# A hybrid decoder layer: projections on two blocks of 512 columns at once, with TensorE in program order

## The chip, the cores and the metric

The kernel runs on one core of a Trainium2 chip. The metric is the device time of one execution in microseconds. The engines are TensorE (PE; its weight loads are shown apart as PEld), VectorE (DVE), ScalarE (ACT), GpSimd (POOL) and SyncE (SP), which here issues nearly all transfers.

## The reference

One decoder layer on 256 tokens with a residual stream of 2048 features, all in float32:

```python
h = h + 0.5 * swiglu(rmsnorm(h, ffn1_norm), ffn1_w_gu, ffn1_w_down)          # width 5632
proj = rmsnorm(h, mix_norm) @ w_in                                            # u | v | z | x,B,C | dt
a_out = chunked_sgu(gelu(u), gelu(v), gm_v_norm, gm_w_s, gm_b_s)              # chunks of 128 tokens
m_out = mamba2_group(z, xbc, dt, conv_w, conv_b, dt_bias, a_log, d, norm)     # conv of 4, scan, gate, norm
h = h + concat([a_out, m_out]) @ w_out
h = h + memory_cross_attention(rmsnorm(h, xa_norm), rmsnorm(mem, mem_norm), w_q, w_kv, w_o)  # 4 heads, 256 memory tokens
h = h + 0.5 * swiglu(rmsnorm(h, ffn2_norm), ffn2_w_gu, ffn2_w_down)
return rmsnorm(h, final_norm)
```

u, v, z and x are 2048 columns each, B and C 1024 each.

## The kernel before

The weights are float32 in HBM and are used once. A tile `raw` of 1 MB (128 partitions, 4 rows of k, 512 columns) is loaded by SyncE; ScalarE casts it into `whi` (float32r, 128x1024 a cast) and VectorE subtracts to get the rest, `wlo`. The operand (the normed stream, or the hidden values) is kept split the same way, high parts of 256 tokens beside low parts, in four tiles named `xt_...`, `hid`, `at` and so on. Each product is three matmuls: high by high, high by low, low by high. There are three buffers for `raw` and four each for `whi` and `wlo`.

`proj_tok` puts tokens on the partitions of the result: one block of 512 columns at a time, one PSUM bank for each of the two token tiles; the operand is the stationary side, the weights the moving one (lines 147 to 149, 128x512). `proj_feat` puts features on the partitions (lines 164 to 167, 128x256): x, B and C of w_in, the queries and the keys. Six PSUM banks serve both as accumulators, two more ("side" tiles) everything else: transposes, the scan's matmuls, logits.

The code is written stage by stage, and a scheduler sets the order of the instructions on every engine when the kernel is built: it may move a matmul ahead of others that stand earlier in the program, where dependences allow. The stages are: FFN 1 in two halves (6 and 5 blocks of gate and up columns, `w_gu`, then `w_dn`); B, C and x of w_in with their convolution (`conv_silu`: VectorE `xin`, four taps on ScalarE and VectorE, ScalarE's silu into `xf`); v, with the scan woven in; u, with `make_mixed`; z; w_out; queries, keys and `attend`; values; w_o; FFN 2 and the final norm.

The places that the text below comes back to:

- `x_tokens(c, xfs)` (line 401) transposes the convolved x of block c back to tokens. It is called after the projection of the next block.
- `scan_start(t, j)` loads `dec` by a broadcast from HBM, subtracts (line 438), takes a minimum, an exponential and multiplies with `scores` (line 446). `scan_apply` does the matmuls `yp` (line 456), `st` and `yo` (line 477).
- `make_mixed` (lines 521, 522): eight matmuls of 128x512, each evacuated by VectorE with the norm's weight.
- `to_operand` (line 192 and after) transposes 512 columns and writes an operand tile, by ScalarE (`hi`) and VectorE (`lo`), when its inputs are ready.
- At the start the stream is loaded by blocks `h0` to `h3` of 512 columns, with a weight tile behind each of the first three, and `first_stats` takes the sums of squares after the first projection.
- At the end `finish(n)` weights block n; the fourth call also takes the norm of each token tile and issues its four stores. The last projection is called with `apart=2`: its last two groups of rows run token tile by token tile.

```python
for n in range(4):
    pd = proj_tok(w_dn, c_from * NC, hts, n * NC, apart=2 if closing and c_to == 11 and n == 3 else 0)
    residual(n, pd, 0.5)
    if c_to == 11:
        done(n)
```

Of the kernel before, what the change touches and what calls it, by code (L numbers as in the profile page):

```python
# [16 lines left out]
P = 128  # L17
D = 2048
S = 256
# [14 lines left out]
KG = 4  # L34
LOG1P_TERMS = 9

# columns of the packed per-partition parameters
# [8 lines left out]
def hybrid_layer(ctx: ExitStack, tc: tile.TileContext, x, mem, w_gu1, w_dn1, w_in, w_s, w_out,  # L46
# [12 lines left out]

    def slot(shape, dtype, name):  # L60
        return big.tile(shape, dtype, name=name, tag="slot")
# [38 lines left out]
    def load(w, r0, n0, pieces=1):  # L100
        raw = wraw.tile([P, KG, NC], F32, name="raw")
        src = w[r0:r0 + KG * P, n0:n0 + NC].rearrange("(k p) n -> p k n", p=P)
        st = KG // pieces
        for j in range(0, KG, st):
            nc.sync.dma_start(out=raw[:, j:j + st, :], in_=src[:, j:j + st, :])
        return raw

    last_hi = [None]

    def split(raw, behind=None):  # L110
        # behind: for each half, instructions of ScalarE and VectorE to queue it behind
        parts = []
        for j in range(0, KG, 2):
            hi = wsp.tile([P, 2, NC], F32R, name="whi")
            lo = wsp.tile([P, 2, NC], F32R, name="wlo")
            with ExitStack() as order:
                for ins in behind[j // 2] if behind else ():
                    order.enter_context(tc.issue_after(ins))
                last_hi[0] = nc.scalar.copy(out=hi, in_=raw[:, j:j + 2, :]).ins  # L119
                nc.vector.tensor_tensor(out=lo, in0=raw[:, j:j + 2, :], in1=hi.bitcast(F32), op=ALU.subtract)  # L120
            parts.append((hi, lo))
        return parts
# [3 lines left out]
    def load_split(w, r0, n0):  # L126
        key = (id(w), r0, n0)
        return split(*ready.pop(key)) if key in ready else split(load(w, r0, n0))

    # Operands in xts: tiles [P, KG, 2 * S] with the high parts of S tokens, then the low parts.  # L130
    def proj_tok(w, r0, xts, n0, apart=0):
        # the last `apart` groups run token tile by token tile
        ps = [mm.tile([P, NC], F32, name="acc") for _ in range(NT)]
        groups = [[g] for g in range(len(xts) - apart)]
        if apart:
            groups.append(list(range(len(xts) - apart, len(xts))))
        for gs in groups:
            parts = {g: load_split(w, r0 + g * KG * P, n0) for g in gs}
            order = [(t, g, k) for g in gs for k in range(KG) for t in range(NT)]
            if len(gs) > 1:  # L140
                order.sort()
            for t, g, k in order:
                hi, lo = parts[g][k // 2]
                first, last = g == 0 and k == 0, g == len(xts) - 1 and k == KG - 1
                xh = xts[g][:, k, t * P:(t + 1) * P]
                xl = xts[g][:, k, S + t * P:S + (t + 1) * P]
                nc.tensor.matmul(ps[t], lhsT=xh, rhs=hi[:, k % 2, :], start=first, stop=False)  # L147
                nc.tensor.matmul(ps[t], lhsT=xh, rhs=lo[:, k % 2, :], start=False, stop=False)  # L148
                nc.tensor.matmul(ps[t], lhsT=xl, rhs=hi[:, k % 2, :], start=False, stop=last)  # L149
        return ps  # L150

    # Features on partitions: two tiles of [P, 2, S], for four groups of 128 features.
    def proj_feat(w, xts, n0):
        ps = [mm.tile([P, 2, S], F32, name="acc") for _ in range(2)]
        for g, xt in enumerate(xts):
            parts = load_split(w, g * KG * P, n0)
            for k in range(KG):
                hi, lo = parts[k // 2]
                first, last = g == 0 and k == 0, g == len(xts) - 1 and k == KG - 1
                for c in range(4):  # L160
                    cs = slice(c * P, (c + 1) * P)
                    o = ps[c // 2][:, c % 2, :]
                    # one accumulation group for both halves of a bank
                    nc.tensor.matmul(o, lhsT=hi[:, k % 2, cs], rhs=xt[:, k, :S], start=first and c % 2 == 0,  # L164
                                     stop=False)
                    nc.tensor.matmul(o, lhsT=hi[:, k % 2, cs], rhs=xt[:, k, S:], start=False, stop=False)  # L166
                    nc.tensor.matmul(o, lhsT=lo[:, k % 2, cs], rhs=xt[:, k, :S], start=False,  # L167
                                     stop=last and c % 2 == 1)
        return ps

# [14 lines left out]
    # 512 columns of NT token tiles -> one split operand tile, scaled per feature  # L185
    def to_operand(srcs, dst, c0=None):
        done = []
        for q in range(0, KG, 2):
            ps = side("tpose").rearrange("p (k s) -> p k s", k=2)
            for k in range(2):  # L190
                for t in range(NT):
                    nc.tensor.transpose(out=ps[:, k, t * P:(t + 1) * P],  # L192
                                        in_=srcs[t][:, (q + k) * P:(q + k + 1) * P], identity=ident)
            if c0 is None:
                hi = nc.scalar.copy(out=dst[:, q:q + 2, :S], in_=ps)
                lo = nc.vector.tensor_tensor(out=dst[:, q:q + 2, S:], in0=ps,
                                             in1=dst[:, q:q + 2, :S].bitcast(F32), op=ALU.subtract)
            else:
                for k in range(2):
                    sc = col[:, c0 + q + k:c0 + q + k + 1]  # L200
                    hi = nc.scalar.activation(dst[:, q + k, :S], ps[:, k, :], AF.Copy, scale=sc)
                    lo = nc.vector.scalar_tensor_tensor(out=dst[:, q + k, S:], in0=ps[:, k, :], scalar=sc,
                                                        in1=dst[:, q + k, :S].bitcast(F32),
                                                        op0=ALU.mult, op1=ALU.subtract)
            done.append((hi.ins, lo.ins))
        return done

    class Normed:
        """The next norm's operand, made chunk by chunk as the residual stream gets ready."""
# [5 lines left out]
        def chunk(self, n):  # L215
            self.operand(n)
            self.stats(n)

        def operand(self, n):
            dst = slot([P, KG, 2 * S], F32R, f"xt_{self.name}{n}")  # L220
            self.xts.append(dst)
            return to_operand([h[n][:, t, :] for t in range(NT)], dst, self.c0 + n * KG)
# [7 lines left out]
    def residual(n, ps, scale):  # L230
        for t in range(NT):
            nc.vector.scalar_tensor_tensor(out=h[n][:, t, :], in0=ps[t], scalar=scale, in1=h[n][:, t, :],
                                           op0=ALU.mult, op1=ALU.add)

# [1 line left out]
    def ffn(nrm, w_gu, w_dn, done, before=None, closing=False):  # L236
        for c_from, c_to in ((0, 6), (6, 11)):
            hts = []
            for c in range(c_from, c_to):
                pg = proj_tok(w_gu, 0, nrm.xts, c * NC)  # L240
                if c == 0 and before is not None:
                    before()
                gs = []
                for t in range(NT):
                    g = half_k(F32, "gate")
                    nc.scalar.activation(g, pg[t], AF.Silu, scale=nrm.rstd[:, t:t + 1])
                    gs.append(g)
                pu = proj_tok(w_gu, 0, nrm.xts, DFF + c * NC)
                for t in range(NT):
                    nc.vector.scalar_tensor_tensor(out=gs[t], in0=pu[t], scalar=nrm.rstd[:, t:t + 1],  # L250
                                                   in1=gs[t], op0=ALU.mult, op1=ALU.mult)
                dst = slot([P, KG, 2 * S], F32R, "hid")
                to_operand(gs, dst)
                hts.append(dst)
            for n in range(4):
                pd = proj_tok(w_dn, c_from * NC, hts, n * NC, apart=2 if closing and c_to == 11 and n == 3 else 0)
                residual(n, pd, 0.5)
                if c_to == 11:
                    done(n)

    n1 = Normed("ffn1", C_FFN1)
    for n in range(4):
        for t in range(NT):
            nc.sync.dma_start(out=h[n][:, t, :], in_=x_v[:, t, n * NC:(n + 1) * NC])
        if n < 3:
# [452 lines left out]
```

## Time and profile before

| | |
|---|---|
| median of 3 runs | 2558.9 us (2558.71 to 2560.08) |
| the profiled execution, span | 2557.8 us |
| TensorE busy | 2539.3 us, 99% |
| VectorE busy | 1375.6 us, 54% |
| ScalarE busy | 1164.2 us, 46% |
| HBM read | 472.57 MB, 186 GB/s over the span |

The span is the time from the first to the last instruction or transfer of one execution, which the profiler recorded; it is 1.1 us under the median of the runs that were timed without it. Matmuls overlap: a shown length holds the filling of the array too, so that the step from one start to the next is what a matmul costs. In a row of the timeline stand the start, the length, the engine, the line of the code, the operation, result and operands, the shape, how many were merged, and in brackets the idle time before it with what ended it.

### The profile page before, as it was taken

The numbers are of one execution on the slowest core, as the hardware profiler recorded it, in microseconds if no ns is written. First come the engines' busy times: TensorE is split into PE (matmuls) and PEld (weight loads), VectorE is DVE, ScalarE is ACT, GpSimd is POOL, SyncE is SP. The second block draws the span as 40 slices with busy tenths as digits, with TensorE's granted clock in tenths as the row PEclk, the third lists the DMA queues.
The fourth block names the chain that finished last, engine by engine and source line by source line (L and its number), as shares of the span: only waits on it lengthen the run. The fifth ranks groups of instructions, "written<-read, shape, count | busy, mean of one in ns | idle before, by whom it ended". The sixth has DMA issues, their size and how long they took to land.

```text
span 2557.8 us, 31301 instructions
## 1 busy us (share of the span) xinstructions
PE 2539.3 (99%) x12990; PEld 2160.8 (84%) x12990; DVE 1375.6 (54%) x1444; ACT 1164.2 (46%) x1391; POOL 19.8 (1%) x44
## 2 busy tenths in 40 slices
PE   8999999999999999999999999999999999999998
PEld 7888888888889998878888999888888888888887
DVE  5445444545557677755555555555554544445454
ACT  5444434444445455445444544444444443344443
POOL 0000000000000000000000000000000000000000
PEclk9999999999999999999999999999999999999999
DMA  6555555555555555545555655455555555555564
GB/s 236 193 183 193 185 197 196 182 191 188 184 175 173 185 189 190 196 158 190 194 185 182 214 180 167 148 181 177 185 187 192 191 187 194 191 191 189 198 192 145
DMA packets 238704, 476.73 MB, mean 186 GB/s; under 512 B 9713, under 2 KB 9873, under 8 KB 237793
## 3 DMA queue, kind: packets, MB, share of 16 engines
q1 hardware_dynamic: 236736, 465.86, 54.2%
q0 software_dynamic: 1680, 8.73, 1.1%
q8 instruction: 101, 1.65, 0.3%
q14 instruction: 43, 0.34, 0.0%
q10 hardware_dynamic: 144, 0.13, 0.0%
HBM read 472.57 MB, written 2.13 MB: 186 GB/s over the span
## 4 chain that ended last, share of the span: by engine, by line
PE 99%; DMA 0%; issue 0%; SPq 0%; ACT 0%; DVE 0%; ACTq 0%; POOLq 0%; POOL 0%
PE acc L147 27%; PE acc L148 27%; PE acc L149 27%; PE acc L164 5%; PE acc L166 5%; PE acc L167 5%; PE tpose L192 2%; PE yp L456 1%; DMA h<-in_x 0%; PE mixed L521 0%; PE o L654 0%; PE o L652 0%; PE scores L443 0%; PE logits L610 0%; PE logits L611 0%
## 5 line engine op out<-in xcount | busy, mean ns | idle before, releaser
L120 DVE TENSOR_TENSOR wlo<-raw,whi 128x1024 fp32r<-128x1024 f32 x880 | 1076.9, 1225 | 1100.6 <-ACT whi L119 1100.3
L119 ACT CAST whi<-raw 128x1024 fp32r<-128x1024 f32 x880 | 927.4, 1054 | 1253.3 <-PE acc L149 1095.8
L148 PE MATMUL acc<-wlo,xt_ffn 128*128 128x512 f32 x1408 | 550.2, 391 | 0.0
L149 PE MATMUL acc<-whi,xt_ffn 128*128 128x512 f32 x1408 | 550.1, 391 | 0.0
L147 PE MATMUL acc<-whi,xt_ffn 128*128 128x512 f32 x1408 | 548.8, 390 | 0.0
L148 PEld LDWEIGHTS acc<-wlo,xt_ffn 128*128 128x128 f32 x1408 | 264.6, 188 | 54.3
L147 PEld LDWEIGHTS acc<-whi,xt_ffn 128*128 128x128 f32 x1408 | 264.6, 188 | 54.3
L149 PEld LDWEIGHTS acc<-whi,xt_ffn 128*128 128x128 f32 x1408 | 264.7, 188 | 53.6
L148 PE MATMUL acc<-wlo,hid 128*128 128x512 f32 x704 | 274.6, 390 | 0.0
L149 PE MATMUL acc<-whi,hid 128*128 128x512 f32 x704 | 274.5, 390 | 0.0
L147 PE MATMUL acc<-whi,hid 128*128 128x512 f32 x704 | 274.0, 389 | 0.0
L148 PEld LDWEIGHTS acc<-wlo,hid 128*128 128x128 f32 x704 | 132.1, 188 | 27.4
L147 PEld LDWEIGHTS acc<-whi,hid 128*128 128x128 f32 x704 | 132.2, 188 | 27.3
L149 PEld LDWEIGHTS acc<-whi,hid 128*128 128x128 f32 x704 | 132.2, 188 | 26.8
L147 PE MATMUL acc<-whi,xt_mix 128*128 128x512 f32 x384 | 151.7, 395 | 0.0
L149 PE MATMUL acc<-whi,xt_mix 128*128 128x512 f32 x384 | 150.9, 393 | 0.0
L148 PE MATMUL acc<-wlo,xt_mix 128*128 128x512 f32 x384 | 150.0, 391 | 0.0
L164 PE MATMUL acc<-xt_mix,whi 128*128 128x256 f32 x512 | 145.5, 284 | 0.0
L166 PE MATMUL acc<-xt_mix,whi 128*128 128x256 f32 x512 | 145.2, 284 | 0.0
L167 PE MATMUL acc<-xt_mix,wlo 128*128 128x256 f32 x512 | 144.8, 283 | 0.0
L164 PEld LDWEIGHTS acc<-xt_mix,whi 128*128 128x128 f32 x512 | 98.2, 192 | 0.6 <-issue 0.4
L166 PEld LDWEIGHTS acc<-xt_mix,whi 128*128 128x128 f32 x512 | 98.2, 192 | 0.2
(237 smaller groups left out, 2827.7 us busy)
## 6 DMA issues: line engine op xcount, KB each, us to landing
raw<-in_w_gu SPq DMA_DIRECT2D x173, 1024.0 KB, 4.8
raw<-in_w_dn SPq DMA_DIRECT2D x88, 1024.0 KB, 5.1
raw<-in_w_in SPq DMA_DIRECT2D x80, 1024.0 KB, 5.1
raw<-in_w_out SPq DMA_DIRECT2D x32, 1024.0 KB, 5.2
raw<-in_w_kv SPq DMA_DIRECT2D x32, 1024.0 KB, 5.4
raw<-in_w_q SPq DMA_DIRECT2D x16, 1024.0 KB, 5.3
raw<-in_w_o SPq DMA_DIRECT2D x16, 1024.0 KB, 5.1
dec<-cum_rows POOLq DMA_DIRECT2D x4, 1024.0 KB, 5.7
```

The costliest lines, as they stand in the source:

```text
L119: last_hi[0] = nc.scalar.copy(out=hi, in_=raw[:, j:j + 2, :]).ins
L120: nc.vector.tensor_tensor(out=lo, in0=raw[:, j:j + 2, :], in1=hi.bitcast(F32), op=ALU.subtract)
L147: nc.tensor.matmul(ps[t], lhsT=xh, rhs=hi[:, k % 2, :], start=first, stop=False)
L148: nc.tensor.matmul(ps[t], lhsT=xh, rhs=lo[:, k % 2, :], start=False, stop=False)
L149: nc.tensor.matmul(ps[t], lhsT=xl, rhs=hi[:, k % 2, :], start=False, stop=last)
L164: nc.tensor.matmul(o, lhsT=hi[:, k % 2, cs], rhs=xt[:, k, :S], start=first and c % 2 == 0, stop=False)
L166: nc.tensor.matmul(o, lhsT=hi[:, k % 2, cs], rhs=xt[:, k, S:], start=False, stop=False)
L167: nc.tensor.matmul(o, lhsT=lo[:, k % 2, cs], rhs=xt[:, k, :S], start=False, stop=last and c % 2 == 1)
L192: nc.tensor.transpose(out=ps[:, k, t * P:(t + 1) * P], in_=srcs[t][:, (q + k) * P:(q + k + 1) * P], identity=ident)
L456: nc.tensor.matmul(yp[:, i, :], lhsT=dec[:, hh, :], rhs=xdt[:, j * 16 + hh, :], start=True, stop=True)
```

## The change

`proj_tok` now takes two blocks of 512 columns at once. For the FFN these are a gate block and its up block, elsewhere neighbours. It holds four accumulators, and a weight tile is 2 rows of k by 1024 columns (still 1 MB). In the first and the last piece the matmuls run token tile by token tile, and each token tile is evacuated (`evac`) as soon as it is complete. `add_proj` does so for the projections into the stream, so two blocks of `h` are completed together.

Every matmul and transpose on TensorE is kept in program order. Matmuls that belong to no projection are put off by `later(fn, by)`: they are emitted after so many further pieces (`step()` at the end of each piece of a projection).

```diff
+    steps, put_off = [0], []
+    def matmul(out, lhsT, rhs, start=False, stop=False):
+        return tc.keep_in_program_order(nc.tensor.matmul(out, lhsT=lhsT, rhs=rhs, start=start, stop=stop))
+    def later(fn, by=1):
+        put_off.append((steps[0] + by, len(put_off), fn))
+    def step(to=None):
+        steps[0] += 1
+        for job in sorted(put_off, key=lambda j: j[:2]):
+            if job[0] <= steps[0] or to == "end":
+                put_off.remove(job)
+                job[2]()
...
-    def proj_tok(w, r0, xts, n0, apart=0):
-        ps = [mm.tile([P, NC], F32, name="acc") for _ in range(NT)]
-        groups = [[g] for g in range(len(xts) - apart)]
...
-                nc.tensor.matmul(ps[t], lhsT=xh, rhs=hi[:, k % 2, :], start=first, stop=False)
-                nc.tensor.matmul(ps[t], lhsT=xh, rhs=lo[:, k % 2, :], start=False, stop=False)
-                nc.tensor.matmul(ps[t], lhsT=xl, rhs=hi[:, k % 2, :], start=False, stop=last)
+    def proj_tok(w, r0, xts, cs, evac, kts=D // P, apart=1):
+        n = kts // KP
+        groups = [[i] for i in range(n - apart)] + [list(range(n - apart, n))]
+        for ng, pieces in enumerate(groups):
+            parts = {i: load_split(w, r0 + i * KP * P, cs) for i in pieces}
+            order = [(t, i, k) for i in pieces for k in range(KP) for t in range(NT)]
+            if ng in (0, len(groups) - 1):
+                order.sort()
+            for t, i, k in order:
...
+                matmul(a, xh, hi[:, 0, :], start=first, stop=False)
+                matmul(a, xh, lo[:, 0, :])
+                matmul(b, xh, hi[:, 1, :], start=first)
+                matmul(b, xh, lo[:, 1, :])
+                matmul(a, xl, hi[:, 0, :], start=False, stop=last)
+                matmul(b, xl, hi[:, 1, :], stop=last)
+                if last:
+                    evac(t, ps[t])
+            step()
...
+    def add_proj(w, r0, xts, scale, done=None, **kw):
+        for n in range(0, 4, 2):
+            def evac(t, ps):
+                for j in range(2):
+                    hh = h[n + j][:, t, :]
+                    nc.vector.scalar_tensor_tensor(out=hh, in0=ps[j], scalar=scale, in1=hh, op0=ALU.mult, op1=ALU.add)
...
+            if done is not None:
+                done(n)
+                done(n + 1)
...
+    first = [(0, 0), (0, 1), (1, 2)]
...
+    for n in range(1, 4):
+        later(lambda n=n: x_operand(n), by=2 * n - 1)
+    for n in range(4):
+        later(lambda n=n: n1.stats(n), by=4 + n)
...
     for c in range(4):
         ps = proj_feat(w_in, nx.xts, X0 + c * NC)
-        if late is not None:
-            x_tokens(*late)
...
+            later(lambda c=c, i0=i0, xf=xf: x_tokens(c, i0, xf), by=1 + i0 // 2)
...
+    for i, (by, to) in enumerate(((3, 7), (7, 10), (13, 17), (17, 21))):
+        later(lambda i=i: scan_start(i // 2, i % 2), by=by)
+        later(lambda i=i: scan_apply(i // 2, i % 2), by=to)
...
+    for g in range(4):
+        later(lambda g=g: make_mixed(g), by=2 + g)
...
-    ffn(n2, w_gu2, w_dn2, finish, closing=True)
+    ffn(n2, w_gu2, w_dn2, finish, {"apart": 2})
+    step("end")
```

`first` says which weight tiles stand behind which block of x at the start: two behind `h0`, one behind `h1`. With `apart=2` the last two pieces (of 2 rows of k each) run token tile by token tile. `operand_later`, new too, puts the transposes of an operand tile off by one piece, half a tile each.

In the order of the instructions this shows at three places. The names with numbers are buffers; `xt_mix_...` are the operand tiles of the mixers' norm.

TensorE at the first block of x, before: the eight transposes stand behind the last matmul of the second block's projection.

```order
L167 MATMUL acc<-xt_mix_5085,wlo 128x256
L401 MATMUL tpose<-ident,xf 128x128 x8
L164 MATMUL acc<-xt_mix_4494,whi 128x256
L166 MATMUL acc<-xt_mix_4494,whi 128x256
L167 MATMUL acc<-xt_mix_4494,wlo 128x256
```

The same now: four transposes stand behind the first piece of the second block's projection (48 matmuls on the first operand tile).

```order
L69 MATMUL acc<-xt_mix_4805,whi 128x256 x2
L69 MATMUL acc<-xt_mix_4805,wlo 128x256
L72 MATMUL tpose<-ident,xf 128x128 x4
L69 MATMUL acc<-xt_mix_4815,whi 128x256 x2
L69 MATMUL acc<-xt_mix_4815,wlo 128x256
```

The transposes moved from the end of the next projection to the end of its first quarter. ScalarE around the same place, now (lines 374 and 378 are the convolution's, 148 the cast, 483 the copy of the transposes):

```order
L374 ACTIVATE cacc<-xin_5168,col 128x256
L148 CAST whi<-raw 128x1024 x2
L378 ACTIVATE xf<-cacc,col 128x256
L374 ACTIVATE cacc<-xin_5169,col 128x256
L374 ACTIVATE cacc<-xin_5167,col 128x256
L148 CAST whi<-raw 128x1024
L378 ACTIVATE xf<-cacc,col 128x256 x2
L374 ACTIVATE cacc<-xin_5168,col 128x256
L483 COPY y_6359<-tpose 128x256
```

Up to the last row this is the order of before; the copies of the transposes have come into it. VectorE at the very end, before (`h_81` to `h_84` are the four blocks of the stream, line 232 the addition, lines 180 and 181 the norm's mean, 679 and 681 the scaling):

```order
L232 SCALAR_TENSOR_TENSOR h_84<-acc,h_84 128x512
L180 TENSOR_REDUCE ms<-ss_f 128x1
L181 TENSOR_SCALAR ms<-ms 128x1
L679 SCALAR_TENSOR_TENSOR h_84<-h_84,rstd_f_19090,fw 128x512
L681 TENSOR_SCALAR h_83<-h_83,rstd_f_19090 128x512
L232 SCALAR_TENSOR_TENSOR h_84<-acc,h_84 128x512
L180 TENSOR_REDUCE ms<-ss_f 128x1
```

And now (lines 291, 223, 224, 770 and 772 are the same five; 764 multiplies the third block with the final norm's weight):

```order
L291 SCALAR_TENSOR_TENSOR h_84<-acc,h_84 128x512
L764 TENSOR_TENSOR h_83<-h_83,fw 128x512
L291 SCALAR_TENSOR_TENSOR h_83<-acc,h_83 128x512
L291 SCALAR_TENSOR_TENSOR h_84<-acc,h_84 128x512
L764 TENSOR_TENSOR h_83<-h_83,fw 128x512
L223 TENSOR_REDUCE ms<-ss_f 128x1
L224 TENSOR_SCALAR ms<-ms 128x1
L772 TENSOR_SCALAR h_83<-h_83,rstd_f_19269 128x512
```

The mean of token tile 0 moved behind the additions of token tile 1. ScalarE at the start, before and then now (line 201, now 242, writes the operand; 217 is a sum of squares):

```order
L201 ACTIVATE xt_ffn_129<-tpose,col 128x256 x3
L119 CAST whi<-raw 128x1024
L201 ACTIVATE xt_ffn_129<-tpose,col 128x256
L119 CAST whi<-raw 128x1024
L201 ACTIVATE xt_ffn_148<-tpose,col 128x256 x3
```

```order
L217 ACTIVATE junk,ss_ffn_111<-h_81 128x512 x2
L242 ACTIVATE xt_ffn_135<-tpose,col 128x256 x3
L217 ACTIVATE junk,ss_ffn_111<-h_82 128x512
L242 ACTIVATE xt_ffn_135<-tpose,col 128x256
L148 CAST whi<-raw 128x1024 x4
```

Sums of squares, the first of `h_82` among them, have moved ahead of the first cast.

More of the change, by code (lines that the diff above doesn't have):

```diff
@@ L153, in proj_feat @@
     def proj_feat(w, xts, n0):
         ps = [mm.tile([P, 2, S], F32, name="acc") for _ in range(2)]
[L155 to L159, printed above, removed]
+        for i in range(D // P // (2 * KP)):
+            raw = wraw.tile([P, 2 * KP, NC], F32, name="raw")
+            nc.sync.dma_start(out=raw, in_=w[2 * i * KP * P:2 * (i + 1) * KP * P, n0:n0 + NC].rearrange(
+                "(k p) n -> p k n", p=P))
+            parts = split(raw.rearrange("p (k j) n -> p k j n", j=2))
+            for k in range(2 * KP):
+                kt = 2 * i * KP + k
+                hi, lo = (x[:, k % 2, :] for x in parts[k // 2])
+                xt = xts[kt // KG][:, kt % KG, :]
+                first, last = kt == 0, kt == D // P - 1
@@ L162, in proj_feat @@
                     o = ps[c // 2][:, c % 2, :]
[L164 to L168, printed above, removed]
+                    matmul(o, hi[:, cs], xt[:, :S], start=first and c % 2 == 0, stop=False)
+                    matmul(o, hi[:, cs], xt[:, S:])
+                    matmul(o, lo[:, cs], xt[:, :S], start=False, stop=last and c % 2 == 1)
+            step()
         return ps
@@ L183, in rstd_of @@
         return r
[L186 to L189, printed above, removed]
-            for k in range(2):
[L191 to L206, printed above, removed]
@@ L208, in hybrid_layer, with operand_later, half, first @@
+    def operand_later(srcs, to, name, c0=None, by=1):
+        def half(q):
+            if q == 0:
+                to.append(slot([P, KG, 2 * S], F32R, name))
+            return to_operand(srcs, to[at], q, c0)
+        at = len(to) + sum(1 for o in owed if o is to)
+        owed.append(to)
+        def first():
+            owed.remove(to)
+            assert len(to) == at
+            half(0)
+            later(lambda: half(2), by=0)
+        later(first, by)
+    owed = []
     class Normed:
@@ L421, in hybrid_layer @@
     dend = small.tile([P, HEADS], F32, name="dend", bufs=1)
-    ecum = small.tile([P, HEADS], F32, name="ecum", bufs=1)
-    nc.scalar.activation(ecum, cum[:, 1, :], AF.Exp)
     scan = {}
@@ L463, in scan_apply @@
             nc.vector.tensor_tensor(out=xdt, in0=xdt, in1=per_head(dend, HD), op=ALU.mult)
-            scan["states"] = states = slot([P, GROUPS, REP * HD], F32, "states")
-            for q in range(4):
-                st = side("st").rearrange("p (g d) -> p g d", g=2)
-                for i in range(2):
-                    g = q * 2 + i
-                    nc.tensor.matmul(st[:, i, :], lhsT=btok[:, g, :], rhs=xdt[:, g * REP:(g + 1) * REP, :],
-                                     start=True, stop=True)
-                nc.any.tensor_copy(out=states[:, q * 2:q * 2 + 2, :], in_=st)
+            later(scan_states, by=2)
         else:
@@ L483, in scan_apply, with scan_states @@
                 nc.vector.tensor_tensor(out=ys, in0=ys, in1=tq, op=ALU.add)
+    def scan_states():
+        scan["states"] = states = slot([P, GROUPS, REP * HD], F32, "states")
+        xdt = scan["xdt0"]
+        for q in range(4):
+            st = side("st").rearrange("p (g d) -> p g d", g=2)
+            for i in range(2):
+                g = q * 2 + i
+                matmul(st[:, i, :], btok[:, g, :], xdt[:, g * REP:(g + 1) * REP, :], start=True, stop=True)
+            nc.any.tensor_copy(out=states[:, q * 2:q * 2 + 2, :], in_=st)
     wst = const.tile([P, 4, P], F32, name="wst")
@@ new lines, in hybrid_layer, with evac @@
+    for hd in (0, 2):
+        vvs = [slot([P, 2, 2, XD], F32R, "vv") for _ in range(2)]
+        def evac(m, ps):
+            for j in range(2):
+                nc.scalar.copy(out=vvs[j][:, m, 0, :], in_=ps[j])
+                nc.vector.tensor_tensor(out=vvs[j][:, m, 1, :], in0=ps[j], in1=vvs[j][:, m, 0, :].bitcast(F32),
+                                        op=ALU.subtract)
+        proj_tok(w_kv, 0, mem_ts, (D + hd * XD, D + (hd + 1) * XD), evac)
+        for j in range(2):
+            for q in range(2):
+                later(lambda hd=hd, j=j, q=q, vv=vvs[j]: weigh(hd + j, vv, q), by=1 + j)
```

415 lines of the change are left out of this document (208 added, 207 removed).

## The prediction

> **What bounds the kernel now.** I read the page first: busy shares, the chain that ended last, the costliest groups.
>
> ```profile
> span 2557.8 us, 31301 instructions
> PE 2539.3 (99%) x12990; PEld 2160.8 (84%) x12990; DVE 1375.6 (54%) x1444; ACT 1164.2 (46%) x1391; POOL 19.8 (1%) x44
> ...
> PE 99%; DMA 0%; issue 0%; SPq 0%; ACT 0%; DVE 0%; ACTq 0%; POOLq 0%; POOL 0%
> ...
> L120 DVE TENSOR_TENSOR wlo<-raw,whi 128x1024 fp32r<-128x1024 f32 x880 | 1076.9, 1225 | 1100.6 <-ACT whi L119 1100.3
> L119 ACT CAST whi<-raw 128x1024 fp32r<-128x1024 f32 x880 | 927.4, 1054 | 1253.3 <-PE acc L149 1095.8
> L148 PE MATMUL acc<-wlo,xt_ffn 128*128 128x512 f32 x1408 | 550.2, 391 | 0.0
> ...
> L148 PEld LDWEIGHTS acc<-wlo,xt_ffn 128*128 128x128 f32 x1408 | 264.6, 188 | 54.3
> ```
>
> TensorE is the chain. VectorE waits for the ScalarE cast, the cast waits for TensorE to release a buffer: both are about half idle, ahead of TensorE. The wide matmul groups have no idle before them. The list of TensorE's own waits has two lines, and only the first is of any size; it belongs to the start.
>
> ```profile
> PE tpose L192 <- DMA h<-in_x: 8.4, 2, 4.7
> PE tpose L626 <- DVE probs L622: 0.2, 1, 0.2
> ```
>
> So little waiting is left to remove. What a matmul costs is read from start to start, since the shown lengths overlap; the timeline, first and last of 55 matmuls:
>
> ```profile
> 599.63 0.39 PE L147 MATMUL acc<-whi,xt_ffn 128*128 128x512 f32 x1
> 599.86 0.39 PE L148 MATMUL acc<-wlo,xt_ffn 128*128 128x512 f32 x1
> 600.09 0.39 PE L149 MATMUL acc<-whi,xt_ffn 128*128 128x512 f32 x1
> ...
> 611.88 0.39 PE L147 MATMUL acc<-whi,xt_ffn 128*128 128x512 f32 x1
> ```
>
> (611.88 − 599.63)/54 = 0.2267 us. The change issues the same matmuls, so what it can alter is this spacing, the stalls in the middle (few, by the list above), the start and the tail.
>
> **The change, part by part.** The FFN, Z, w_out, w_o and the second half of w_kv: blocks of 1024 columns, 1 MB a piece, four accumulators. A piece is 24 matmuls, 24 × 0.2267 = 5.44 us, and needs two casts (2.1 us) and two subtractions (2.45 us): cover of more than half, as before. I take 0. The cover is the four wlo/whi buffers; should an evacuation at the end of a projection delay casts by more than about 3 us (5.44 − 2.45), this zero is gone (a rival below). The FFN's loads as two transfers of half the size and SP's longer list change nothing while the casts wait for TensorE and not for data.
>
> *X stage.* x_tokens(c) no longer stands one whole projection after its convolution, but one piece of the next one after it (its second half two pieces). TensorE now obeys program order, so it cannot run other matmuls meanwhile. Timeline after the first X projection, TensorE, then VectorE and ScalarE, then the transposes:
>
> ```profile
> 870.87 0.28 PE L164 MATMUL acc<-xt_mix,whi 128*128 128x256 f32 x1
> ...
> 872.19 0.28 PE L167 MATMUL acc<-xt_mix,wlo 128*128 128x256 f32 x1
> 872.31 0.28 PE L164 MATMUL acc<-xt_mix,whi 128*128 128x256 f32 x1
> ...
> 872.51 1.14 DVE L303 TENSOR_TENSOR xin<-acc,rstd_b 128x256 f32<-128x256 f32 x3
> ...
> 878.27 2.46 DVE L310 SCALAR_TENSOR_TENSOR cacc<-xin,col,cacc 128x256 f32<-128x256 f32 x6
> ...
> 878.93 1.05 ACT L119 CAST whi<-raw 128x1024 fp32r<-128x1024 f32 x1 [0.62 <-PE acc L166]
> 880.36 0.92 ACT L312 ACTIVATE xf<-cacc,col 128x256 f32<-128x256 f32 x2 [0.38 <-DVE cacc L310]
> ...
> 896.08 1.03 PE L401 MATMUL tpose<-ident,xf 128*128 128x128 f32 x8
> ```
>
> Narrow matmuls start every (872.31 − 870.87)/12 = 0.12 us. The projection ends at 872.31; its last matmul is the one of 872.19. The first half of x_tokens needs the xf of two convolutions: the second is the first of the pair at 880.36 and is done at about 880.36 + 0.51 = 880.87, 8.56 us after the projection's end. Before, the transposes came at 896.08, with 15 us to spare. Now TensorE reaches them after one piece, 48 × 0.12 = 5.76 us, and waits 8.56 − 5.76 = 2.8 us, three times; the fourth time V's first piece lies ahead, 5.44 us, and it waits 3.1. The order on ScalarE around it is unchanged, so I keep 8.56. Sum 3 × 2.8 + 3.1 = **+11.5** (8 to 14: each chain a microsecond shorter or longer). The second half, after two pieces, finds its xf ready.
>
> *V and U.* Program order now places scores, yp, st, yo and mixed at stated pieces. Before, this stage ran almost without a hole: in the window 1073.42 to 1096.08 (22.66 us) stand 33 wide matmuls (7.48 us), 32 passes of yp (3.5), 16 of yo, 16 of mixed and 8 transposes (0.9).
>
> ```profile
> 1073.42 3.52 PE yp L456 x32
> 1076.93 0.92 PE yo L477 x4
> 1078.79 1.73 PE yo L477 x8
> ...
> 1093.79 0.86 PE mixed L521 x2
> ```
>
> With 1.73/8 = 0.216 a yo pass and 0.86/2 = 0.43 a mixed pass that is 7.48 + 3.5 + 3.5 + 6.9 + 0.9 = 22.3, so only 0.4 us of hole. New holes I expect at two places. First, in U's second piece mixed needs both side banks, one of them held by the scores of the last scan step until VectorE has done the multiplication; the second half of mixed also waits for the first to be evacuated, and that stands on VectorE behind a dec subtraction, which waits for a broadcast that starts only when a slot is free:
>
> ```profile
> L438 DVE TENSOR_TENSOR dec<-dec,cum 128x2048 f32<-128x2048 f32 x4 | 9.2, 2292 | 0.5 <-DMA dec<-cum_rows 0.5
> L522 DVE TENSOR_TENSOR v<-mixed,wn 128x512 f32<-128x512 f32 x8 | 5.3, 684 | 2.2 <-PE mixed L521 2.2
> ...
> dec<-cum_rows POOLq DMA_DIRECT2D x4, 1024.0 KB, 5.7
> ```
>
> Landing 5.7 + subtraction 2.3 + evacuation 0.7 = 8.7 us after the slot is free, against one piece and a mixed, about 6.3: 2.4, with queueing 3. Second, the piece where the last mixed, yp and yo come together takes eight side tiles of 0.69 us of VectorE each, by two banks: about 2, and 1 for smaller ones. Less the about 2 us of holes that V and U have today: **+4** (0 to 8).
>
> *C0 and attention.* cum's copies now hold both side banks ahead of b_tokens: +0.2. Probabilities turn two pieces later than their logits: the 0.2 us wait of the list and some smaller ones go, −1 (−1 to 0).
>
> *Start.*
>
> ```profile
> 4.66 2.30 PE L192 MATMUL tpose<-ident,h 128*128 128x128 f32 x8 [4.66 <-DMA h<-in_x]
> ...
> 8.57 1.05 ACT L119 CAST whi<-raw 128x1024 fp32r<-128x1024 f32 x1 [0.21 <-DMA raw<-in_w_gu]
> ...
> 10.72 1.49 PE L192 MATMUL tpose<-ident,h 128*128 128x128 f32 x4 [3.76 <-DMA h<-in_x]
> ...
> 11.86 1.20 PE L147 MATMUL acc<-whi,xt_ffn 128*128 128x512 f32 x2
> ...
> 13.29 0.63 PE L149 MATMUL acc<-whi,xt_ffn 128*128 128x512 f32 x1
> 13.71 0.63 PE L148 MATMUL acc<-wlo,xt_ffn 128*128 128x512 f32 x1
> ...
> 15.33 0.39 PE L147 MATMUL acc<-whi,xt_ffn 128*128 128x512 f32 x1
> 15.56 0.39 PE L148 MATMUL acc<-wlo,xt_ffn 128*128 128x512 f32 x1
> ...
> 8.00:11.00 3.00, 0.28 (x1) 0.18 (x1) 2.08 (x4) 2.78 (x4) 0.00 (x0) 1.00 1.05 399
> ```
>
> The second block of x lands at 10.72 today, behind one weight tile; now behind two. 1.05 MB more at 399 GB/s is 2.6 us: 13.4. On ScalarE the sum of squares of that block now stands ahead of the fourth xt_ffn activation and of the first cast. So the first cast, at 8.57 today, begins at 13.4 + 0.8 + 0.5 = 14.7, and the first matmul at about 15.8 instead of 11.86: +3.9. TensorE is slow then (13.29 to 13.71 is 0.42, 0.23 from 15.3 on), as today, and four subtractions in a row follow: **+5** in all (2 to 7).
>
> *Tail.*
>
> ```profile
> 2546.37 7.21 SPq L684 DMA_DIRECT2D out<-h  x8
> 2548.11 0.39 PE L149 MATMUL acc<-whi,hid 128*128 128x512 f32 x1
> ...
> 2548.54 0.69 DVE L232 SCALAR_TENSOR_TENSOR h<-acc,h 128x512 f32<-128x512 f32 x1 [1.77 <-PE acc L149]
> ```
>
> Today token tile 0 is finished under the last matmuls and four of the eight stores go out early; the last is issued at 2546.37 + 7.21 = 2553.58, 5.2 us after the last matmul's slot (2548.11 + 0.23). Now two blocks end together, and on VectorE and ScalarE tile 0's row sum stands behind tile 1's additions and squares, which wait for the last matmul: two additions (1.4), a multiplication, two squares, then two chains of reduce, power and scaling, four multiplications, and all eight stores behind them. By my list the last store is issued about 8.3 us after: **+3.1** (2 to 5).
>
> Sum: 11.5 + 4 + 0.2 − 1 + 5 + 3.1 = +22.8. On the span of 2557.8 that is 2580.6; the median of the runs shown, 2558.9, is 1.1 above the span: 2581.7, so **2582 us**. With each part's bounds (8, 0, −1, 2, 2 and 14, 8, 0, 7, 5): 2570 to 2593.
>
> **Rivals.**
>
> *Faster: a weight kept in the array.* Today one of three matmuls has the stationary operand of its predecessor (L147 to L148); now four of six. If a repeat saved the part of the slot that does not scale with columns, 0.2267 − 2 × (0.2267 − 0.12) = 0.0133 us, then 9024 wide matmuls (by the code: the two FFNs 6336, V, U and Z 1152, w_out 768, values and w_o 768) × 0.0133 × (4/6 − 1/3) = 40 us would go and the time be about 2582 − 40 = 2542. Against it: L147 to L148 (0.23) repeats, L148 to L149 (0.23) doesn't, with the same step, and L148 has its own 1408 loads. I give it 0.05. It decides as soon as a repeat saves over 9 ns. The Trainium skill, "TensorE: Matmul & The Clock Gate", Part 2, step ①, says that decoupled loading allows to load once and multiply repeatedly, which speaks for this case; the equal steps show no gain from it here.
>
> *The X waits are hidden.* If the convolution's chain runs 3 us faster when its pieces come sooner, 11.5 goes: about 2570. For it: ScalarE idles before most casts; against: six VectorE steps of 2.46 and a cast stand in the chain itself. 0.10.
>
> *The clock falls after each X wait.* TensorE ran at 0.42 a wide matmul until 15.3, after 3.8 us of idleness ending at 10.72. If each of four waits of about 3 us set it back for the same 4.6 us (10.72 to 15.3), half of that is lost: 4 × 2.3 = 9, about 2591. 0.10. The Trainium skill, same page, "HAM oscillation — how this bites in real kernels", puts the limit at idle gaps of about 3.4 us; by it gaps of 2.8 and 3.1 just escape, and the sum stays.
>
> *Casts late at every projection.* One microsecond at each of the 44 pairs of blocks: +44, about 2626. Against: the half-idle ScalarE and VectorE. 0.05. It decides when evacuation and cast together exceed 5.44 us.
>
> *Nothing:* the new waits are as small as the old: about 2559. 0.04, as the list of TensorE's waits has no such gap to trade.
>
> **How the numbers follow.** Forecast 0.66, the others 0.05, 0.10, 0.10, 0.05, 0.04. The range 2566 to 2597 takes in the forecast, the hidden X waits and the clock, 0.86, less some edges. 0.2%, 5 us, is about what a measurement can tell from no change here: slower 0.91, same 0.04, faster 0.05.
>
> **What would show it.** In the list of TensorE's waits: tpose on xf from ScalarE, four times, 2.5 to 3.5 us; mixed and yo on VectorE, some 5 us; first wide matmul near 15.8; last store issued 8 us after the last matmul; wide spacing still 0.2267; no wait in the FFN. I'm wrong if the spacing shrinks, if a wait recurs at every pair of blocks, or if TensorE falls back to 0.42 a matmul in the X stage.

## The result and the profile after

The changed kernel takes 2578.4 us (median of 4 runs, 2575.8 to 2579.7) against 2559.2 before: ratio 1.0073, interval 1.0058 to 1.0087. It is 19 us slower; 23 had been forecast. The profiled execution, the fastest of the four, has a span 16.1 us longer than before's:

```profile
span 2573.9 us, 31721 instructions
...
PE 2536.2 (99%) x12990; PEld 2166.1 (84%) x12990; DVE 1376.7 (53%) x1445; ACT 1160.0 (45%) x1389; POOL 20.3 (1%) x44
...
PE 97%; DMA 1%; DVE 1%; issue 0%; ACT 0%; SPq 0%; DVEq 0%; POOLq 0%; POOL 0%; ACTq 0%
```

TensorE issues as many instructions as before and is busy 3 us less, so the 16 us are not more work. The list of TensorE's waits, which had 8.6 us in it, shows where it stands idle now:

```profile
PE acc L69 <- ACT whi L148: 8.7, 1, 8.7
PE tpose L72 <- ACT xf L378: 7.0, 4, 1.9
PE tpose L72 <- DMA h<-in_x: 4.8, 2, 4.4
PE mixed L69 <- DVE v L604: 2.9, 1, 2.9
PE tpose L72 <- ACT cumt L443: 0.7, 1, 0.7
PE acc L69 <- DVE wlo L149: 0.5, 1, 0.5
PE dt L69 <- DVE dt L406: 0.4, 1, 0.4
PE yo L69 <- DVE yoff L547: 0.2, 1, 0.2
```

None is in the FFN's steady part. First the X stage, as the timeline shows it at its third wait (TensorE):

```profile
934.61 0.27 PE L72 MATMUL tpose<-ident,xf 128*128 128x128 f32 x1
936.73 0.55 PE L72 MATMUL tpose<-ident,xf 128*128 128x128 f32 x3 [1.85 <-ACT xf L378]
```

The first transpose, of the first convolution, runs; the second then stands 2.0 us at the head of TensorE's queue until ScalarE has written the other `xf`. Four such waits give the 7.0 us. Something can follow them. In the table of stretches the columns are stretch, length, TensorE's busy time and count, granted clock, share of the DMA engines, GB/s; the first two rows lie around the second wait, the others around the third:

```profile
907.16:910.57 3.41, 1.75 (x15) 1.00 0.81 291
910.57:913.99 3.42, 3.23 (x27) 1.00 0.32 62
934.47:937.88 3.41, 1.56 (x14) 1.00 0.41 169
937.88:941.29 3.41, 3.41 (x18) 0.50 0.71 210
```

The clock was granted at half for 3.4 us (937.9 to 941.3) behind the third wait, and behind none of the other three. That cost 1.7 us. How often it comes differs from run to run: the four runs show mean clocks of 0.998, 0.997, 0.996 and 0.997 with spans of 2573.9, 2577.8, 2577.2 and 2575.8, where every run of the kernel before has 0.999. The profiled execution is thus at the good end. What decides it is told in the last section.

The start (ScalarE and TensorE), against a first cast at 8.57 and a first matmul at 11.86 before:

```profile
13.55 0.63 ACT L217 ACTIVATE junk<-h 128x512 f32<-128x512 f32 x1 [4.93 <-DMA h<-in_x]
...
14.18 0.45 ACT L242 ACTIVATE xt_ffn<-tpose,col 128x256 fp32r<-128x256 f32 x1
14.53 3.87 ACT L148 CAST whi<-raw 128x1024 fp32r<-128x1024 f32 x4
...
15.62 0.79 PE L69 MATMUL acc<-whi,xt_ffn 128*128 128x512 f32 x1 [8.66 <-ACT whi L148]
```

ScalarE waits 4.93 us for the second block of x, for a sum of squares that nobody needs yet, and the casts wait behind it. The broadcast behind U's first piece (GpSimd, VectorE, TensorE):

```profile
1069.62 0.53 POOL L508 DMA_DIRECT2D dec<-cum_rows  x1 [3.53 <-PE yp L69]
...
1076.53 2.29 DVE L513 TENSOR_TENSOR dec<-dec,cum 128x2048 f32<-128x2048 f32 x1 [1.17 <-DMA dec<-cum_rows]
1078.73 0.68 DVE L604 TENSOR_TENSOR v<-mixed,wn 128x512 f32<-128x512 f32 x1
...
1079.47 1.12 PE L69 MATMUL mixed<-v,wss 128*128 128x512 f32 x2 [2.88 <-DVE v L604]
```

yp frees the slot at 1069.6, the broadcast lands 6.9 us later, VectorE subtracts, and only then evacuates the bank that the second `mixed` waits for. And the tail (TensorE, VectorE, SyncE):

```profile
2560.62 0.61 PE L69 MATMUL acc<-whi,hid 128*128 128x512 f32 x2
...
2561.05 1.29 DVE L291 SCALAR_TENSOR_TENSOR h<-acc,h 128x512 f32<-128x512 f32 x2 [3.27 <-PE acc L69]
...
2563.14 0.16 DVE L223 TENSOR_REDUCE ms<-ss_f 128x1 f32<-128x4 f32 x1
...
2564.70 5.16 SPq L775 DMA_DIRECT2D out<-h  x8
```

The last matmul is the second of the pair, at 2560.85; its slot ends at about 2561.1. The reduction for token tile 0 comes 2.1 us after that, and the last store is issued at 2569.86, 8.8 us after it (5.2 before).

### The profile page after: what moved, and what is told of

Read it like the earlier page. It is cut to its first block, busy times and chain, and to the rows that moved or that the text cites. A ratio compares the mean times of both kernels' runs of the same rounds, so it can differ in the third digit from the quotient of the medians.

```text
span 2573.9 us, 31721 instructions
## 1 busy us (share of the span) xinstructions
PE 2536.2 (99%) x12990; PEld 2166.1 (84%) x12990; DVE 1376.7 (53%) x1445; ACT 1160.0 (45%) x1389; POOL 20.3 (1%) x44
## 4 chain that ended last, share of the span: by engine, by line
PE 97%; DMA 1%; DVE 1%; issue 0%; ACT 0%; SPq 0%; DVEq 0%; POOLq 0%; POOL 0%; ACTq 0%
PE acc L69 93%; PE tpose L72 2%; PE yp L69 1%; PE logits L69 0%; PE o L69 0%; DMA raw<-in_w_gu 0%; DMA dec<-cum_rows 0%; PE mixed L69 0%; ACT whi L148 0%; DVE cacc L376 0%; DVE wlo L149 0%; PE dt L69 0%; PE st L69 0%; PE scores L69 0%; PE yo L69 0%
## 5 line engine op out<-in xcount | busy, mean ns | idle before, releaser
L69 PE MATMUL acc<-whi,xt_ffn 128*128 128x512 f32 x2816 | 880.1, 391 | 8.7 <-ACT whi L148 8.7
L69 PE MATMUL acc<-whi,hid 128*128 128x512 f32 x1408 | 436.8, 390 | 0.0
L69 PE MATMUL acc<-xt_mix,whi 128*128 128x256 f32 x1024 | 187.3, 285 | 0.0
L69 PEld LDWEIGHTS acc<-whi,xt_mix 128*128 128x128 f32 x768 | 144.2, 188 | 30.3 <-ACT whi L148 0.5
L69 PEld LDWEIGHTS acc<-xt_mix,wlo 128*128 128x128 f32 x512 | 98.9, 193 | 0.0
L69 PE MATMUL acc<-memt,whi 128*128 128x256 f32 x512 | 92.9, 284 | 0.0
L69 PE MATMUL acc<-xt_xa,whi 128*128 128x256 f32 x512 | 92.9, 284 | 0.0
L69 PEld LDWEIGHTS acc<-wlo,xt_mix 128*128 128x128 f32 x384 | 72.1, 188 | 15.4 <-issue 0.7
L69 PE MATMUL acc<-whi,at 128*128 128x512 f32 x256 | 80.3, 391 | 0.0
L69 PEld LDWEIGHTS acc<-xt_xa,whi 128*128 128x128 f32 x512 | 79.8, 192 | 0.1
```

Source lines behind the costliest of these rows:

```text
L69: return pe(nc.tensor.matmul(out, lhsT=lhsT, rhs=rhs, start=start, stop=stop))
```

## The experiments

Each starts from the changed kernel, whose median is 2578.4 us; medians of the kernel before beside them were 2559.4 to 2559.6.

**The X waits.** One piece more:

```diff
-            later(lambda c=c, i0=i0, xf=xf: x_tokens(c, i0, xf), by=1 + i0 // 2)
+            later(lambda c=c, i0=i0, xf=xf: x_tokens(c, i0, xf), by=2 + i0 // 2)
```

> x_tokens is put off by one piece more (2 and 3 instead of 1 and 2). The theory that TensorE waits there for the convolution's second xf: the four waits of transposes on xf (7.0 us in the list, 7.7 by the steps) fall to nothing, with them the stretch of slow clock behind one of them (1.6 us), and the time is about 2578.4 - 9 = 2569, with spans closer together than the 3.9 us of the changed kernel's runs. The rival that the piece only moves the wait (ScalarE's copies of the transposes then come late for V, or the tmp tiles run out): the waits come back at other lines, and the time stays above 2575.

Measured 2567.6 us (2566.8 to 2570.6), 10.8 less. The list has no wait on `xf` any more, and none in its place. The spread only narrowed to 3.8 us: `mixed` still waits, 3.2 us here, and in this profile the slow clock followed that wait. The opposite, no piece between the projection and its transposes:

> The first half of x_tokens directly behind its projection: four waits of about 7.7 us (the whole convolution's chain) instead of 2. If the clock falls after every wait over some length, each of the four is followed by 3.4 us at half clock (1.7 us lost): span 2573.9 + 4 x 5.7 + 3 x 1.7 = 2602. If the slow stretch comes by chance, one or two of four: 2598. The clock by stretches of the four waits tells.

One profiled run: 2604.2 us, span 2602.3, the number of the case with slow clock after every wait. The waits and the four slow stretches:

```profile
PE tpose L72 <- ACT xf L378: 24.6, 8, 3.5
...
881.50:888.50 7.00, 4.28 (x21) 0.52 0.43 147
912.30:922.60 10.30, 6.34 (x29) 0.51 0.32 103
946.50:953.30 6.80, 3.85 (x17) 0.51 0.47 154
980.60:987.40 6.80, 5.36 (x14) 0.51 0.78 299
```

Each transposing place now has a pair of waits, 3.1 us each on average, and each pair brings the clock down, for two or three times 3.4 us. So the number is in part luck: the waits are 24.6 us by the list where 4 x 7.7 = 30.8 were expected, and the four slow stretches hold 19.8 us of matmuls, some 9.9 us lost, where 4 x 1.7 = 6.8 were.

**The start.** In `split` the last cast is remembered, and:

```diff
-        later(lambda n=n: n1.stats(n), by=4 + n)
+        def late_stats(n=n):
+            with tc.issue_after(last_hi[0]):
+                n1.stats(n)
+        later(late_stats, by=4 + n)
```

> Only the sums of squares of the first norm are queued behind the last cast issued, so on ScalarE the first cast no longer stands behind the sum of squares of the second block of x. Theory: the first wide matmul starts at about 10 to 11 us instead of 15.6, and 5 us go: about 2573.4. Rival (the first casts wait for weights, or the second block of x is needed at the third piece anyway): the first matmul is early but TensorE waits later, and 2 us or less go.

Measured 2573.2 us (2569.9 to 2574.7), 5.2 less. The first matmul has moved six microseconds ahead, and in the trace the 1000th wide matmul (246.8 for 251.6 us) is still 4.9 ahead:

```profile
9.59 0.80 PE L69 MATMUL acc<-whi,xt_ffn 128*128 128x512 f32 x1 [2.52 <-ACT whi L148]
```

**The tail.** The last two blocks are finished token tile by token tile, from the evacuation itself:

```diff
     def evac(t, ps):
         for j in range(2):
             nc.vector.scalar_tensor_tensor(out=h[n + j][:, t, :], ...)
+        if tok is not None and n == 2:
+            tok(t)       # squares of blocks 2 and 3, norm, scaling and four stores of token tile t
```

> Only the end: the last two blocks are finished token tile by token tile, the first under the last matmuls. Theory: from the last matmul's start to the span's end 13.1 us become about 10.2 (last store issued some 5.7 us after the matmul instead of 9), so -2.9: about 2575.5. Rival (the stores' completion, not their issue, sets the end): less than 1 us.

Measured 2574.9 us (2570.9 to 2575.9), 3.5 less. Four stores are issued under the last matmuls again, and the last at 2565.02, 5.6 us after the last slot's end (2559.4) for 8.8, so 3.1 us less in the trace:

```profile
2557.80 7.22 SPq L789 DMA_DIRECT2D out<-h  x8
...
2558.93 0.61 PE L69 MATMUL acc<-whi,hid 128*128 128x512 f32 x2
```

**mixed.** One piece later (`by=3 + g` for `by=2 + g`):

> Only mixed one piece later, behind the last dec's exponential. Theory: the wait of mixed on VectorE (2.9 us) goes, span -2.9: about 2571 if one stretch of slow clock falls in the X stage as in the profile shown, up to 2575 with more of them. Rival (VectorE is full there, and the wait moves to yo or to the next mixed): span unchanged within 1 us, and yo waits 2 us or more.

A miss for both: one profiled run, 2575.9 us, span 2574.0, with two slow stretches in the X stage. `mixed` still waits 1.8 us, yo no more than before:

```profile
PE mixed L69 <- DVE v L604: 1.8, 1, 1.8
...
PE yo L69 <- DVE yoff L547: 0.2, 1, 0.2
```

Later, the evacuation stands behind VectorE's minimum (`dec<-dec,lim`) and a `wlo`. Putting the waiting work off does not help where the work ahead of it on VectorE slides too.

**A repeated stationary operand.** The rival with the highest price:

```diff
-                matmul(a, xh, hi[:, 0, :], ...); matmul(a, xh, lo[:, 0, :]); matmul(b, xh, hi[:, 1, :], ...)
-                matmul(b, xh, lo[:, 1, :]); matmul(a, xl, hi[:, 0, :], ...); matmul(b, xl, hi[:, 1, :], ...)
+                matmul(a, xh, hi[:, 0, :], ...); matmul(a, xl, hi[:, 0, :]); matmul(a, xh, lo[:, 0, :], ...)
+                matmul(b, xl, hi[:, 1, :], ...); matmul(b, xh, hi[:, 1, :]); matmul(b, xh, lo[:, 1, :], ...)
```

> The six matmuls of a k row and token tile in another order: high, low, high for the first block, low, high, high for the second, so that the stationary operand repeats once instead of four times in six. Theory (a repeat saves nothing): spacing of wide matmuls 0.2267 us, time within 2 us of the changed kernel's 2578. Rival (a repeated operand saves 13 ns of the slot): 3 of 6 of 9024 matmuls by 13.3 ns is 60 us, 2638.

Measured 2583.8 us (2578.6 to 2584.7): 5 more, not 60. The timeline in the FFN, first of this kernel (one repeat in six), then of the changed one (four in six):

```profile
611.78 0.39 PE L69 MATMUL acc<-wlo,xt_ffn 128*128 128x512 f32 x1
612.00 0.62 PE L69 MATMUL acc<-whi,xt_ffn 128*128 128x512 f32 x2
612.46 0.39 PE L69 MATMUL acc<-wlo,xt_ffn 128*128 128x512 f32 x1
```

```profile
610.55 0.39 PE L69 MATMUL acc<-wlo,xt_ffn 128*128 128x512 f32 x1
610.77 0.84 PE L69 MATMUL acc<-whi,xt_ffn 128*128 128x512 f32 x3
611.45 0.39 PE L69 MATMUL acc<-wlo,xt_ffn 128*128 128x512 f32 x1
```

Three steps in 0.68 us, four in 0.90: 0.226 us either way. The list of waits shows where a part of the 5 us came from:

```profile
PE mixed L69 <- DVE v L604: 4.6, 1, 4.6
PE yp L69 <- DVE v L604: 1.1, 1, 1.1
```

That is 2.8 us more than in the changed kernel; the profiled run is 2.8 us longer in span, and its mean clock is 0.997, in the others 0.995 and 0.996. VectorE there does a `wlo` and the minimum (`dec<-dec,lim`) ahead of the evacuation that `mixed` waits for; why the scheduler set them so is open. The "within 2 us" that was expected was missed for these waits, not for the spacing.

**Program order.** The pin left out, everything else kept:

```diff
     def pe(ins):
-        return tc.keep_in_program_order(ins)
+        return ins
```

> The changed kernel without the pin on program order: the scheduler may move matmuls. Built so, it sets the first transposes of xf where they are now and the other three some 16 matmuls (1.9 us) later, and the second matmul of each mixed pair some matmuls later, but the second block of x's transposes ahead of the first matmul. Theory (program order costs the waits, two blocks at once costs nothing): the waits on xf (7.0 us) and on mixed (2.9 us) go, the tail and start stay: about 2578.4 - 10 = 2568 (2565 to 2573). Rival (the order by hand is worth something elsewhere, as the smaller holes in attention and the FFN, some 4 us, suggest): these come back and it ends at 2572 or more.

Measured 2562.6 us (2561.3 to 2565.1), 15.8 less, more than either case had.

```profile
PE tpose L72 <- DMA h<-in_x: 11.2, 2, 6.5
PE mixed L69 <- DVE v L604: 1.2, 1, 1.2
PE tpose L72 <- DVE xt_ffn L243: 0.2, 1, 0.2
```

The scheduler puts other matmuls into the X waits and most of `mixed`'s; with the waits go the slow stretches. The start's loss has another name and stays in part (the 1000th wide matmul is 2.4 us later than before, 4.1 in the changed kernel); the tail stays whole (8.8 us to the last store). Ratio to the kernel before 1.0012 (1.0003 to 1.0022): two blocks at once, without the pin, cost about 3 us (1 to 6), with that start and tail in it.

**The mends together.**

> Four mends at once: x_tokens one piece later; mixed one piece later; the first sums of squares behind the last cast issued; the finishing of the last two blocks token tile by token tile. By the steps of the profile: -9 (X waits and slow clock), -2.9 (mixed), -5 (start), -2.9 (tail), together about -20 of the median of 2578.4: 2558.5, within 0.2% of the kernel before (2559.2); by the span 2573.9 - 19 = 2555. If the gains overlap or the waits move on, 2563 or more.

Measured 2556.2 us (2555.5 to 2558.5, 10 runs), 22 less than the change, ratio to before 0.9988 (0.9978 to 0.9997). The gains of the single mends (10.8, 5.2, 3.5 and, from one run, 2.5) add up to 22.0; `mixed` still waits 1.7 us. The mean clock is 0.999 again in nine of the ten runs. Then the cause of `mixed`'s wait taken at the root:

```diff
-    for i, (by, to) in enumerate(((3, 7), (7, 10), (13, 17), (17, 21))):
+    for i, (by, to) in enumerate(((3, 7), (7, 10), (13, 16), (16, 21))):
```

> The mends of all_four, but mixed where the change has it and instead the scan's third application and fourth start one piece sooner (16 for 17), so that the broadcast's slot is free one piece sooner; b_tokens of the second block one piece later. Theory (the wait of mixed is the broadcast: 6.9 us to land, then a subtraction of 2.3 and an evacuation, all counted from the moment that yp frees the slot): mixed's wait, 1.7 us in all_four, falls under 0.5, and the 0.7 us wait on cumt goes: 2556.2 - 2 = about 2554, and faster than the kernel before by 0.2%. Rival (VectorE's own load in this stretch is what mixed waits for): mixed still waits 1.5 us or more, 2556.

Measured 2555.9 us (2555.0 to 2556.6, 11 runs), ratio to before 0.9986 (0.9977 to 0.9995); against all_four no difference that counts.

```profile
PE acc L69 <- ACT whi L148: 2.5, 1, 2.5
PE mixed L69 <- DVE v L614: 1.0, 1, 1.0
PE cps L72 <- DVE btok L473: 0.6, 1, 0.6
```

`mixed` waits 1.0, neither under 0.5 nor 1.5: the broadcast was a part of it, two `wlo` on VectorE ahead of the evacuation the rest. The broadcast also landed sooner here, after 4.8 us for 6.6 in all_four, so the shorter wait is not the earlier start's alone. The wait on cumt came back as one of cps on btok.

> The same numbers and mends without the pin on program order. The scheduler then sets the transposes of the second block of x ahead of the first matmul, which waits for it until about 13.4 us; the rest of the order is nearly that of scan_sooner. Theory (once the numbers are right the pin is worth only the start): 4 us more than scan_sooner, about 2558. Rival (the scheduler's freedom also fills holes that the numbers leave): about the same as scan_sooner, 2555 or less.

Measured 2556.8 us (2555.8 to 2557.2, 11 runs), ratio 0.9989 (0.9981 to 0.9998), 0.9 above scan_sooner where 4 or none were expected: the start has 11.0 us of waits instead of 8.0, and the holes in the middle, 2.2 us by scan_sooner's list, are gone. Both theories hold, and nearly cancel.

## Why the prediction was right, and where it was off

The bound was right: no spacing changed, and the 16 us of the profile are holes in TensorE's queue, one slow stretch and the two ends, nearly all where the steps put them. The sizes of the parts were less right than the total. Both kernels have 9024 wide matmuls, stage by stage in the same order, so that the start of the n-th can be compared. The 1000th, in FFN 1, starts 4.1 us later than before (251.6 for 247.6). The rest of FFN 1 wins back 1.2. Up to V's first matmul 8.7 are lost, in V, U and Z 4.4 (1.7 of them the fourth X wait). The two products of w_out win 1.0, the stretch from there to the last of w_o 2.3. FFN 2 is the same, and from the last matmul on 3.4 are lost.

That the median came within 4 us of the forecast is in part luck: the X waits were put 3.8 us too high and the middle wins 4.4 where 1 was forecast, but the slow clock, worth 1.7 us here and more in the other runs by their mean clocks, was left out of the sum.

- **X stage**, forecast +11.5: the four waits are 7.7 us from slot to slot (7.0 in the list, which counts from the shown ends), and one slow stretch of 1.7 us comes with them. The experiment's 10.8 us hold both. The step that was off is the start of the convolution, taken as fixed at 0.2 us after the projection's end, 872.31. It needs only the first of the two accumulators, which is complete six matmuls before the end; before, VectorE was just then at a `wlo`, until 872.54:

```profile
871.31 1.23 DVE L120 TENSOR_TENSOR wlo<-raw,whi 128x1024 fp32r<-128x1024 f32 x1 [1.66 <-ACT whi L119]
```

In the changed kernel (VectorE, ScalarE, TensorE):

```profile
876.38 1.15 DVE L369 TENSOR_TENSOR xin<-acc,rstd_b 128x256 f32<-128x256 f32 x3
...
884.23 0.91 ACT L378 ACTIVATE xf<-cacc,col 128x256 f32<-128x256 f32 x2 [0.39 <-DVE cacc L376]
...
882.66 0.27 PE L72 MATMUL tpose<-ident,xf 128*128 128x128 f32 x1
```

From the first `xin` to the second `xf` (884.23 + 0.51 = 884.74) it takes 8.36 us, as in the kernel before (872.51 to 880.87). But the piece of 48 matmuls ahead of the transposes began at 882.66 − 5.76 = 876.90, half a microsecond after `xin`, not 0.2 before it. With that, and the first transpose, which does not wait, each of the first three waits is 2.0 us and not 2.8. The fourth is 1.7 and not 3.1: there the chain itself took 7.7 us.
- **The clock after X waits**, a rival of 0.10 at +9: it is real, but at one of four waits in the profile, for 3.4 us and not 4.6, worth 1.7 us. TensorE's fall to half speed in the X stage was named as a sign of being wrong, and there it came. By the mean clocks it makes up much of the difference between the profiled execution (+16.1) and the medians (+19.2). The 4.6 us at the start were no measure of it: the eight transposes of 4.66, ahead of the idleness, took 0.29 us each already, where those of 896.08 took 0.13.
- **Start**, forecast +5: the first matmul at 15.62 for a forecast 15.8; 4.1 us by the 1000th matmul, 5.2 us by its experiment.
- **Tail**, forecast +3.1: 8.8 us to the last store for a forecast 8.3; 3.5 us by its experiment.
- **V and U**, forecast +4: `mixed` waits 2.9 us by the very chain that was named, forecast 3. Five profiled kernels have the change's numbers and order of VectorE there; the broadcast lands after 5.6, 6.9, 7.1, 7.2 and 7.6 us, and `mixed` waits 1.6, 2.9, 3.1, 3.2 and 3.6: the landing less 4.0 each time. The second place, mixed with yp and yo, waits 0.2 us for a forecast 2: there VectorE kept up. Without the X wait, V, U and Z lose 2.7 us.
- **C0**, +0.2: a wait of 0.7 on cumt and one of 0.4 on dt.
- **Attention**, −1: the wait on the probabilities is gone from the list, and the stage wins 2.3, outside the −1 to 0 that was given. Why it wins so much, no experiment took apart.
- **FFN**, 0: no wait of TensorE there, as said, and FFN 2 is the same up to its last matmul. FFN 1 and w_out win 1.2 and 1.0 us that the sum did not have; the cause stays open.
- The **repeated operand** and the **late casts** are ruled out by the equal spacing and the list of waits. That X waits would be **hidden** fell with the four waits.

## What to carry to other kernels

When an engine that is already the bound is given a fixed order, price each put-off instruction by its input's chain, counted from the moment at which the chain really starts, against the work that stands between; a number too small by one piece here cost four times over. Look at the two ends apart: doubling a block doubles what has to be finished after the last matmul, and an early, unneeded reduction can hold the first cast. A wait in the middle can cost a second time through the clock: 1.9 us of waiting, 1.7 us more behind it. Here the fixed order cost 15.8 us over the scheduler's while its numbers were too small. With them mended the two orders end 0.9 us apart, and the fixed one is 0.14% faster than the kernel before.

## What the hardware showed

Waits of TensorE far below 3.4 us can halve its clock. Over the profiles of this study, of twenty X waits of 1.3 to 1.9 us (five kernels with the change's numbers there) seven were followed by 3.4 us at half clock; of five waits of `mixed` of 2.9 to 4.6 us all but the shortest; of five of 1.0 to 1.8 us none. The Trainium skill, "TensorE: Matmul & The Clock Gate", section "HAM oscillation — how this bites in real kernels", warns of idle gaps above about 3.4 us; here 1.85 us sufficed where they lay well.

What "well" means can be read from the record of the clock. In all profiles here, every slow stretch away from the ends starts a whole number of times 3.413 us after the moment at which the clock first came to full, and lasts one, two or three times that. So the span falls into fixed windows of 3.413 us. The seven X waits of 1.85 us that lie whole within one window were followed by half clock in the next; the eight such waits that a boundary cuts in two, and the five shorter ones, were not. The rows shown with the result are four of these windows: the second wait leaves 1.75 us of work in its window, the third 1.56. Counted over all windows at full clock, by the shown lengths of the matmuls, none with 1.78 us of idleness or less was followed by half clock, and of the sixteen with 1.85 or more all but one were (it had 1.848). The wait of `mixed` of 2.9 us that cost nothing lay across a boundary, 1.2 and 1.6 us to each side. Within a slow stretch less idleness kept the clock down (0.84 us once, 1.29 once). In the six profiles with the change's loads at the start the first full clock comes at 18.2 to 21.6 us, so the boundaries lie elsewhere in each run; that the times of one kernel differ for this reason is argued, not shown.
